# A denoising backbone of two layers on one core: buffers and order of its modulation start, and one weighing run per four attention units

## The chip, the cores and the metric

The kernel runs on one core of one Trainium2 chip. The metric is device time in microseconds (us) of one execution; the median of several runs is told. The engines are TensorE (PE, its weight loads PEld), VectorE (DVE), ScalarE (ACT), GpSimd (POOL) and SyncE (SP), whose queue issues the DMAs here.

## What is computed

The reference runs two layers over 512 latent tokens and 256 context tokens of width 1024, all in float32:

```python
for i in range(DEPTH):
    even = i % 2 == 0
    sh1, sc1, g1, sh2, sc2, g2 = adaln_params(s_x, ada_w[i], ada_b[i])
    h_x = modulate(rms_norm(x, norm1_g[i]), sh1, sc1)
    ...
    if even:
        y_x, y_c = even_mixer(h_x, h_c, attn_w_in[j], ...)   # attention of 12 heads, and Fourier mixing
    else:
        y_x = conformer_conv(h_x, *conv_args)
    x = x + g1 * y_x
    x = x + g2 * sq_relu_mlp(modulate(rms_norm(x, norm2_g[i]), sh2, sc2), mlp_w1[i], mlp_w2[i])
```

`adaln_params` is a product of a conditioning vector with a 1024 x 6144 matrix; `rms_norm` divides by the root of the mean square; attention has 12 query heads on 4 key heads, 512 queries against 768 keys. Only the latent stream is returned.

## The kernel before, in words

Products are made from a high and a low half of each operand, three matmuls for one (`three`, `products`). A weight block of 128 x 2048 comes by DMA into a raw tile of the pool `wraw` (two buffers); its high half is a rounding copy (ACT, line 164 or 363, or POOL, 155 or 962), its low half a subtraction (DVE 158 or 167, POOL 963). `pin` keeps an instruction in program order on its engine; all of the code around the change is pinned, so each engine works in the order in which the code stands.

**The start** (lines 331 to 560). The modulation for layer 0 comes from eight blocks `ar0` to `ar7` (`load_ada`, 339), which alternate between the pool `araw` (two buffers) and `wraw`; between them SP issues the two halves of the latents `xx` and the first two weight blocks (345 to 351). A conditioning step n is `cond_sum` (matmuls 376 over two of the blocks), `cond_copy` (ACT 382), `cond_flip` (transposes 387) and `cond_mods` (six to eight small DVE operations, 395 to 401). Three sides are normed: the context (0) and the two halves of the latents (1, 2). For each: `square` (ACT 406), `fold` (DVE 410, 411), `total` (PE 416), `root` (DVE 422, then Ln and Exp on ACT 423, 424), `newton` (DVE 429 to 431), and then for each of eight row tiles `scaled` (DVE 440), `high` (ACT 444), `low` (DVE 448). `step(side, w, kt, half)` is the projection of one row tile, six matmuls (line 327). The order of it all is written out by hand from line 465 on.

**Attention** (884 to 1023). There are 48 units, each one head and 128 queries; n counts scores and m = n - 3 what is worked off. In an iteration stand: the scores of unit n (PE 572, 574) into one of two banks `sc`, the maximum (DVE 577, 578); the reciprocal and the scaling of unit n - 1's shares (DVE 589, POOL 590); perhaps a `piece` of a weight block (POOL 962, 963); the transposes of unit m (PE 928) and their copies (ACT 933; for odd units the second on DVE, 935); the exponent of unit n with its sum (ACT 584); perhaps a gemv `row` (DVE 231) for later modulations, at the units of `ROWS_AT`; and perhaps weighing. Four units make a group of six weighing steps (`weigh`, PE 946, two matmuls each), put into a list behind the fourth unit. From iteration 12 on, every even m takes three steps from the list. A group's last step is followed by its copy out (ACT 952, DVE 953). The data of two rows is one DMA into `wraw` (`load_rows`, SP 970), whose buffers hold the last two weight blocks until their eight pieces are done.

After attention come the output projection, the MLP, the convolution layer and its MLP, with TensorE all but fully busy.

Of the kernel before, what the change touches and what calls it, by code (L numbers as in the profile page):

```python
# [66 lines left out]
ROWS_AT = (20, 22, 26, 28, 30, 32, 33, 34, 36, 38, 40, 41, 42, 44, 45, 46)  # L67
# [8 lines left out]
def build(tc, xT, ctxT, vec, gbc, rope, dft, dft64, eye, ada1, adat,  # L76
# [211 lines left out]
    with ExitStack() as e1:  # L288
# [27 lines left out]
        def split_k(w):  # L316
            return w.rearrange("p e (k n) -> p e k n", k=4)
# [13 lines left out]
        with ExitStack() as e0:  # L331
            p0 = e0.enter_context(tc.tile_pool(name="p0", bufs=1, side=right, reuse_waits='tile'))
            araw = e0.enter_context(tc.tile_pool(name="araw", bufs=2, side=right, reuse_waits='tile'))
# [5 lines left out]
            def load_ada(n):  # L339
                for k in range(len(araws), n):  # L340
                    a = (araw, wraw)[k % 2].tile([P, WB], F32, name=f"ar{k}", tag="raw")
                    nc.sync.dma_start(a, ada1[k])
                    araws.append(a)
# [36 lines left out]
            def cond_copy(n):  # L380
                sa[n] = p0.tile([P, 512], F32, name="sa", tag="sa", bufs=2)
                pin(nc.scalar.activation(sa[n], pa[n], AF.Copy))
# [30 lines left out]
            def total(slot, a):  # L413
                ps = mbank(slot)[:, :H]
                for i in range(2):
                    pin(nc.tensor.matmul(ps, lhsT=ones, rhs=a[:, i], start=i == 0, stop=i == 1))
                return ps

            def root(ps):
                v = p0.tile([P, H], F32, name="rs_v", tag="rs_v", bufs=2)  # L420
                y = p0.tile([P, H], F32, name="rs_y", tag="rs_y", bufs=2)
                pin(nc.vector.tensor_scalar(v, ps, 1.0 / D, EPS, ALU.mult, ALU.add))
                pin(nc.scalar.activation(y, ps, AF.Ln, bias=eps, scale=1.0 / D))
                pin(nc.scalar.activation(y, y, AF.Exp, scale=-0.5))
                return v, y

# [61 lines left out]
            ps = total(2, b0)  # L488
            cond_copy(1)
            cond_flip(1)  # L490
            cond_mods(1)
            w0 = split_k(ws.take())
            for t in range(4):
                w_high(t)
                pin(sides[0].high(t))
                w_low(t)
                pin(sides[0].low(t))
                step(0, w0, t, 0)
                if t == 1:
                    vy = root(ps)  # L500
                if t == 2:
                    r0 = newton(*vy)
            cond_sum(2, range(8))
            for t in range(4):
                pin(sides[1].scaled(t, r0))
            c0 = square(sides[2].src, 0)
            for t in range(2):
                pin(sides[1].high(t))
            c1 = square(sides[2].src, 4)
            for t in range(2, 4):  # L510
                pin(sides[1].high(t))
            for t in range(4):
                pin(sides[1].low(t))
            cond_copy(2)
            fold(c0, c1)
# [4 lines left out]
            ps = total(3, c0)  # L520
            for t in range(4, 8):
                pin(sides[0].scaled(t, rc))
            for t in range(2, 4):
                step(1, w0, t, 0)
            vy = root(ps)
            w_high(4)
# [6 lines left out]
            cond_sum(3, range(8))  # L533
            cond_copy(3)
# [349 lines left out]
        with ExitStack() as ea:  # L884
# [95 lines left out]
            for n in range(len(units) + AHEAD):  # L980
# [9 lines left out]
                if on and ws.later and m % 2 == 0:  # L990
                    piece()
# [18 lines left out]
                if m in ROWS_AT:  # L1010
                    row()
                if not on:
                    for _ in range(2):
                        if work:
                            weigh(*work.pop(0))
                elif m % 2 == 0:
                    for _ in range(3):
                        if work:
                            weigh(*work.pop(0), True)
# [548 lines left out]
```

## Time and profile before

| | us |
|---|---|
| median of 3 runs (lowest, highest) | 1182.0 (1181.2, 1183.33) |
| the profiled execution | 1180.84 |
| its span in the trace | 1179.1 |
| busy: PE, DVE, ACT, POOL | 1157.3, 762.6, 493.1, 168.7 |
| mean granted TensorE clock | 0.998 of full speed |

In the rows further below a line gives its start, its length, the engine, the source line, what is written from what, and how many instructions are merged in it; in brackets stands how long the engine sat idle before it and what ended that. A weighing step of two matmuls shows as four records. PE's lengths overlap, so distances are best taken from start to start.

### The profile page before, as it was taken

Reading aid. Unit: us, or ns where it says so; the run is one execution under the profiler, and the core shown is the slowest. Engines: PE = TensorE matmul, PEld = TensorE weight load, DVE = VectorE, ACT = ScalarE, POOL = GpSimd, SP = SyncE. Lnnn points to the kernel's source line nnn. Section 1 sums busy time; section 2 is a strip of 40 time slices with the busy share of each in tenths; the row PEclk is TensorE's granted clock in tenths of the full one; section 3 lists DMA queues with packets and bytes.
Section 4 is the critical chain, followed back from the end, with each engine's and each line's share of the span. In section 5 each row is a group of like instructions: output and inputs, shape, how many; then the busy total and the mean of one; then the engine's idle time right before and its main releaser. Section 6 shows DMA issues by size and latency. Waiting matters only on the chain.

```text
span 1179.1 us, 16124 instructions
## 1 busy us (share of the span) xinstructions
PE 1157.3 (98%) x6362; PEld 976.4 (83%) x6362; DVE 762.6 (65%) x1370; ACT 493.1 (42%) x883; POOL 168.7 (14%) x198
## 2 busy tenths in 40 slices
PE   6999999999999999999999999999999999999998
PEld 3688776779988888888889988989988888888887
DVE  4986768878976765665646999899753443443431
ACT  5463787745532331332334423777531331332320
POOL 0202367620000000000011148700000000000000
PEclk9999999999999999999999999999999999999999
DMA  9522103365476455555521425332233223322301
GB/s 373 190 72 62 47 14 131 112 263 198 140 257 246 170 190 211 190 184 197 198 92 68 148 76 190 123 113 103 96 120 107 90 89 107 107 80 99 108 18 54
DMA packets 25339, 160.21 MB, mean 136 GB/s; under 512 B 2608, under 2 KB 5680, under 8 KB 6832
## 3 DMA queue, kind: packets, MB, share of 16 engines
q1 hardware_dynamic: 25264, 159.19, 37.7%
q8 instruction: 50, 0.82, 0.3%
q14 instruction: 25, 0.20, 0.0%
HBM read 157.08 MB, written 2.10 MB: 135 GB/s over the span
## 4 chain that ended last, share of the span: by engine, by line
PE 88%; DVE 7%; ACT 2%; issue 1%; DMA 1%; SPq 1%; POOL 0%; DVEq 0%; ACTq 0%
PE mm L192 25%; PE mm L193 25%; PE mm L191 25%; PE sc L327 3%; PE mm L1219 3%; DVE sm L577 3%; PE po L327 2%; PE po L946 1%; DMA ar<-in_ada 1%; ACT p L584 1%; PE tp L928 1%; PE tp L657 1%; PE sc L572 1%; DVE sm L578 0%; PE sc L574 0%
## 5 line engine op out<-in xcount | busy, mean ns | idle before, releaser
L192 PE MATMUL mm<-act,w 128*128 128x512 f32 (+1 forms) x992 | 338.2, 342 | 0.6 <-DVE act L1401 0.3
L193 PE MATMUL mm<-act,w 128*128 128x512 f32 (+1 forms) x992 | 337.6, 341 | 0.0
L191 PE MATMUL mm<-act,w 128*128 128x512 f32 (+1 forms) x992 | 337.1, 342 | 0.0
L164 ACT ACTIVATE w<-raw 128x1024 fp32r<-128x1024 f32 (+1 forms) x168 | 158.0, 970 | 232.7 <-PE mm L193 205.0
L191 PE MATMUL mm<-f,w 128*128 128x512 f32 (+1 forms) x560 | 207.8, 371 | 0.0
L192 PE MATMUL mm<-f,w 128*128 128x512 f32 (+1 forms) x560 | 207.7, 371 | 0.0
L193 PE MATMUL mm<-f,w 128*128 128x512 f32 (+1 forms) x560 | 207.7, 371 | 0.0
L192 PEld LDWEIGHTS mm<-act,w 128*128 128x128 f32 x992 | 187.8, 190 | 22.7 <-DVE act L1401 1.4
L191 PEld LDWEIGHTS mm<-act,w 128*128 128x128 f32 x992 | 187.2, 190 | 22.3 <-ACT act L1411 0.7
L193 PEld LDWEIGHTS mm<-act,w 128*128 128x128 f32 x992 | 187.8, 190 | 21.1
L167 DVE TENSOR_TENSOR w<-raw,w 128x1024 fp32r<-128x1024 f32 (+2 forms) x168 | 179.5, 1094 | 36.0 <-ACT w L164 27.4
L1107 DVE SCALAR_TENSOR_TENSOR x<-mm,mods,x 128x512 f32<-128x512 f32 (+1 forms) x82 | 55.8, 684 | 170.7 <-PE mm L193 169.8
L1161 DVE TENSOR_TENSOR rsq<-relu 128x512 f32<-128x512 f32 (+1 forms) x76 | 45.6, 606 | 122.8 <-ACT relu L1158 122.8
L1158 ACT ACTIVATE relu<-mm 128x512 f32<-128x512 f32 (+1 forms) x76 | 40.2, 529 | 196.6 <-PE mm L193 194.8
L191 PEld LDWEIGHTS mm<-f,w 128*128 128x128 f32 x560 | 105.5, 188 | 18.3
L192 PEld LDWEIGHTS mm<-f,w 128*128 128x128 f32 x560 | 105.5, 188 | 18.2
L193 PEld LDWEIGHTS mm<-f,w 128*128 128x128 f32 x560 | 105.5, 188 | 17.9
L231 DVE SCALAR_TENSOR_TENSOR gv<-gv,sbc 128x1024 f32<-128x1024 f32 x80 | 96.6, 1225 | 6.1 <-DMA gv<-in_adat 6.1
L167 POOL TENSOR_TENSOR w<-raw,w 128x1024 fp32r<-128x1024 f32 x12 | 29.9, 2515 | 404.4 <-ACT w L164 404.3
L1208 DVE SCALAR_TENSOR_TENSOR sb<-u,vecs,sb 128x512 f32<-128x512 f32 x112 | 75.2, 747 | 0.0
L590 POOL TENSOR_SCALAR p<-p,sm 128x768 f32<-128x768 f32 x48 | 58.8, 1225 | 52.0 <-DVE sm L589 42.0
L584 ACT ACTIVATE p<-sc,sm,rq 128x768 f32<-128x768 f32 x48 | 47.8, 995 | 14.4 <-DVE sm L589 9.7
(235 smaller groups left out, 1283.7 us busy)
## 6 DMA issues: line engine op xcount, KB each, us to landing
raw<-in_w SPq DMA_DIRECT2D x64, 1024.0 KB, 4.8
gv<-in_adat SPq DMA_DIRECT2D x40, 1024.0 KB, 5.1
raw<-in_pw SPq DMA_DIRECT2D x12, 1024.0 KB, 4.9
w<-in_diag SPq DMA_DIRECT2D x8, 1152.0 KB, 5.6
ar<-in_ada SPq DMA_DIRECT2D x8, 1024.0 KB, 10.1
raw<-in_w_in SPq DMA_DIRECT2D x6, 1024.0 KB, 4.9
raw<-in_w_out SPq DMA_DIRECT2D x4, 1024.0 KB, 4.8
xx<-in_xT SPq DMA_DIRECT2D x2, 1024.0 KB, 10.7
```

What stands on the lines that cost most here:

```text
L164: hi = nc.scalar.activation(w[:, 0, r], raw[:, r], AF.Copy)
L167: eng.tensor_tensor(w[:, 1, r], raw[:, r], w[:, 0, r].bitcast(F32), ALU.subtract)
L191: nc.tensor.matmul(ps, lhsT=whi, rhs=xhi, start=first, stop=False)
L192: nc.tensor.matmul(ps, lhsT=whi, rhs=xlo, start=False, stop=False)
L193: nc.tensor.matmul(ps, lhsT=wlo, rhs=xhi, start=False, stop=last)
L231: i = nc.vector.scalar_tensor_tensor(r, r, 1.0, sbc, ALU.mult, ALU.mult, accum_out=mod(l, j, t))
L327: i = nc.tensor.matmul(ps, lhsT=a, rhs=w[:, e, k], start=first, stop=last)
L584: held(on, nc.scalar.activation(p, sc[:, :NK], AF.Exp, bias=sm[:, 1:2], scale=r, accum_out=sm[:, 2:3]))
L590: held(on, nc.gpsimd.tensor_scalar(p, p, sm[:, 3:4], 0.0, ALU.mult, ALU.add))
L1107: nc.vector.scalar_tensor_tensor(xs, ps, mod(l, j, t), xs, ALU.mult, ALU.add)
L1161: nc.vector.tensor_tensor(s, r, r, ALU.mult)
L1208: tap = nc.vector.scalar_tensor_tensor(vs if j == TAPS - 2 else a, u[:, t, j:j + S], w[j], a, ALU.mult, ALU.add)
```

## The change

Three edits. First, the pool `araw` gets a third buffer, and of the eight modulation blocks only 1 and 5 go to `wraw`, so that the first weight block has a `wraw` buffer of its own. Second, the order of the start: `root` is cut into `root_sum` (DVE) and `root_log` (ACT); the first root's sum stands right behind its total, and its Ln, Exp and `newton` behind the first step's loop; two weight high halves stand ahead of that loop and each further one two parts ahead; the `scaled` and `high` of side 1 alternate, the second square comes behind the low halves, `fold` behind `cond_mods(2)`, `total(3)` behind one more part of the step, and `w_high(4)` behind the last `cond_sum`. Third, in attention the weighing list is emptied at every m with m % 4 == 1 (at m = 9 the four steps left, then six each time) in place of three steps at every even m; the eight pieces stand at m = 9, 10, 12 to 22 in place of 10 to 24; and the sixteen rows shift to later units.

```diff
@@ -64,7 +64,8 @@
 SLOTS = ((4, 5, 0, 1, 2, 3), (4, 5, 0, 1), (4, 5, 2, 3))
 PAIRS = (4, 5, 0, 1, 2, 3)
 STEADY = 12
-ROWS_AT = (20, 22, 26, 28, 30, 32, 33, 34, 36, 38, 40, 41, 42, 44, 45, 46)
+ROWS_AT = (22, 24, 26, 28, 30, 32, 34, 36, 38, 40, 42, 44, 45, 46, 46, 47)
+PIECES_AT = (9, 10, 12, 14, 16, 18, 20, 22)
 GV_UP = 4
 GV_OUT = 1
 FOURIER_AT = (-1, 1, 3, 5)
@@ -330,7 +331,7 @@
 
         with ExitStack() as e0:
             p0 = e0.enter_context(tc.tile_pool(name="p0", bufs=1, side=right, reuse_waits='tile'))
-            araw = e0.enter_context(tc.tile_pool(name="araw", bufs=2, side=right, reuse_waits='tile'))
+            araw = e0.enter_context(tc.tile_pool(name="araw", bufs=3, side=right, reuse_waits='tile'))
             cx = p0.tile([P, KT, C], F32, name="cx")
             nc.sync.dma_start(ident, eye)
             nc.sync.dma_start(cx, ctxT)
@@ -338,7 +339,7 @@
 
             def load_ada(n):
                 for k in range(len(araws), n):
-                    a = (araw, wraw)[k % 2].tile([P, WB], F32, name=f"ar{k}", tag="raw")
+                    a = (wraw if k in (1, 5) else araw).tile([P, WB], F32, name=f"ar{k}", tag="raw")
                     nc.sync.dma_start(a, ada1[k])
                     araws.append(a)
 
@@ -416,13 +417,20 @@
                     pin(nc.tensor.matmul(ps, lhsT=ones, rhs=a[:, i], start=i == 0, stop=i == 1))
                 return ps
 
-            def root(ps):
+            def root_sum(ps):
                 v = p0.tile([P, H], F32, name="rs_v", tag="rs_v", bufs=2)
                 y = p0.tile([P, H], F32, name="rs_y", tag="rs_y", bufs=2)
                 pin(nc.vector.tensor_scalar(v, ps, 1.0 / D, EPS, ALU.mult, ALU.add))
+                return v, y
+
+            def root_log(ps, vy):
+                v, y = vy
                 pin(nc.scalar.activation(y, ps, AF.Ln, bias=eps, scale=1.0 / D))
                 pin(nc.scalar.activation(y, y, AF.Exp, scale=-0.5))
                 return v, y
+
+            def root(ps):
+                return root_log(ps, root_sum(ps))
 
             def newton(v, y):
                 r = xp.tile([P, H], F32, name="rstd", tag="rstd", bufs=3)
@@ -486,44 +494,42 @@
             fold(b0, b1)
             cond_sum(1, range(8))
             ps = total(2, b0)
+            v1 = root_sum(ps)
             cond_copy(1)
             cond_flip(1)
             cond_mods(1)
             w0 = split_k(ws.take())
+            w_high(0)
+            w_high(1)
             for t in range(4):
-                w_high(t)
                 pin(sides[0].high(t))
+                if t < 2:
+                    w_high(t + 2)
                 w_low(t)
                 pin(sides[0].low(t))
                 step(0, w0, t, 0)
-                if t == 1:
-                    vy = root(ps)
-                if t == 2:
-                    r0 = newton(*vy)
+            vy = root_log(ps, v1)
+            r0 = newton(*vy)
             cond_sum(2, range(8))
             for t in range(4):
                 pin(sides[1].scaled(t, r0))
+                pin(sides[1].high(t))
             c0 = square(sides[2].src, 0)
-            for t in range(2):
-                pin(sides[1].high(t))
-            c1 = square(sides[2].src, 4)
-            for t in range(2, 4):
-                pin(sides[1].high(t))
             for t in range(4):
                 pin(sides[1].low(t))
+            c1 = square(sides[2].src, 4)
             cond_copy(2)
-            fold(c0, c1)
             for t in range(2):
                 step(1, w0, t, 0)
             cond_flip(2)
             cond_mods(2)
-            ps = total(3, c0)
+            fold(c0, c1)
             for t in range(4, 8):
                 pin(sides[0].scaled(t, rc))
-            for t in range(2, 4):
-                step(1, w0, t, 0)
+            step(1, w0, 2, 0)
+            ps = total(3, c0)
+            step(1, w0, 3, 0)
             vy = root(ps)
-            w_high(4)
             r1 = newton(*vy)
             for t in range(4):
                 pin(sides[2].scaled(t, r1))
@@ -531,6 +537,7 @@
             for t in range(4):
                 pin(sides[2].low(t))
             cond_sum(3, range(8))
+            w_high(4)
             cond_copy(3)
             step(2, w0, 0, 0)
             cond_flip(3)
@@ -987,7 +994,7 @@
                 if last is not None:
                     ready[n - 1] = shares(*last, on)
                     last = None
-                if on and ws.later and m % 2 == 0:
+                if m in PIECES_AT:
                     piece()
                 if m < 0:
                     continue
@@ -1007,16 +1014,15 @@
                     place_query(2, 2 + PLACE_AT.index(m), False)
                 if m == ROWS_AT[0] - 2:
                     load_rows()
-                if m in ROWS_AT:
+                for _ in range(ROWS_AT.count(m)):
                     row()
                 if not on:
                     for _ in range(2):
                         if work:
                             weigh(*work.pop(0))
-                elif m % 2 == 0:
-                    for _ in range(3):
-                        if work:
-                            weigh(*work.pop(0), True)
+                elif m % 4 == 1:
+                    while work:
+                        weigh(*work.pop(0), True)
                 if m % 4 == 3:
                     work += [(pair, half, kt) for kt in range(6)]
             for w_ in work:
```

## Rows read from the trace of the kernel before

**Rows 1.** Windows: length, PE, PEld, DVE, ACT, POOL busy (instructions), clock, DMA share, GB/s.
```profile
260.00:280.00 20.00, 20.00 (x132) 18.37 (x131) 16.10 (x26) 7.13 (x11) 0.00 (x0) 1.00 0.59 211
...
800.00:1179.00 379.00, 375.76 (x1934) 323.12 (x1932) 170.98 (x251) 119.82 (x183) 0.00 (x0) 1.00 0.26 89
```

**Rows 2.** Timeline of the start, TensorE and VectorE, 24 to 56 us.
```profile
24.24 3.09 PE L327 MATMUL po<-w,chl 128*128 128x512 f32 x12 [1.01 <-ACT chl L444]
...
32.20 1.92 PE L376 MATMUL tp<-ar,sT 128*32 128x512 f32 x16
...
34.53 1.22 DVE L410 TENSOR_TENSOR sq<-sq 128x1024 f32<-128x1024 f32 x1
35.79 0.69 DVE L411 TENSOR_TENSOR sq<-sq 128x512 f32<-128x512 f32 x1
...
39.75 0.42 DVE L422 TENSOR_SCALAR rs_v<-sc 128x256 f32<-128x256 f32 x1
...
43.62 0.73 PE L327 MATMUL sc<-w,act 128*128 128x512 f32 x2 [0.64 <-ACT act L444]
...
50.25 5.60 PE L327 MATMUL po<-w,chl 128*128 128x512 f32 x24
```

**Rows 3.** Chain that ended last: start, length, engine and line; copies of the start.
```profile
27.12 0.52 ACT w L363
27.64 0.40 ACT chl L444
```

**Rows 4.** Timeline of the start, the late loads and their last reader.
```profile
16.36 14.62 SPq L342 DMA_DIRECT2D ar<-in_ada x4
...
41.05 1.92 PE L376 MATMUL tp<-ar,sT 128*32 128x512 f32 x16
```

**Rows 5.** Timeline of attention: weighing runs, one unit, one wait for a bank.
```profile
161.44 1.52 PE L946 MATMUL po<-PT,vS 128*64 128x256 f32 x12
...
167.62 0.50 PE L572 MATMUL sc<-kA,qT 128*128 128x512 f32 x1
...
168.42 0.82 PE L928 MATMUL tp<-ident,p 128*128 128x128 f32 x6
...
168.69 0.96 DVE L577 TENSOR_REDUCE sm<-sc 128x1 f32<-128x768 f32 x1 [1.81 <-PE sc L574]
...
169.00 0.48 PE L572 MATMUL sc<-kA,qT 128*128 128x512 f32 x1
...
169.96 0.99 ACT L584 ACTIVATE p<-sc,sm,rq 128x768 f32<-128x768 f32 x1 [0.30 <-PE sc L574]
...
170.66 1.52 PE L946 MATMUL po<-PT,vS 128*64 128x256 f32 x12
...
172.11 0.50 PE L572 MATMUL sc<-kA,qT 128*128 128x512 f32 x1
...
215.64 0.99 ACT L584 ACTIVATE p<-sc,sm,rq 128x768 f32<-128x768 f32 x1 [0.73 <-DVE sm L589]
...
216.78 0.19 PEld L572 LDWEIGHTS sc<-kA,qT 128*128 128x128 f32 x1 [0.18 <-ACT p L584]
...
244.27 3.34 PE L946 MATMUL po<-PT,vS 128*64 128x256 f32 x28
```

**Rows 6.** Chain that ended last: two weighing runs one round apart.
```profile
195.40 1.45 PE po L946 x12
...
204.61 1.45 PE po L946 x12
```

**Rows 7.** Timeline of attention: a gemv row, and a weight piece.
```profile
195.95 1.21 DVE L231 SCALAR_TENSOR_TENSOR gv<-gv,sbc 128x1024 f32<-128x1024 f32 x1
...
163.10 0.61 POOL L962 CAST w<-raw 128x512 fp32r<-128x512 f32 x1
...
163.80 1.28 POOL L963 TENSOR_TENSOR w<-raw,w 128x512 fp32r<-128x512 f32 x1
```

**Rows 8.** Timeline behind attention: the first residual add.
```profile
254.18 0.75 DVE L1107 SCALAR_TENSOR_TENSOR x<-mm,mods,x 128x512 f32<-128x512 f32 x1 [0.80 <-DMA x<-in_xT]
```

## The prediction

> **What bounds the kernel now.** I read the windows first: TensorE is busy for 375.76 of the last 379 us [rows 1], so nothing behind attention can give time back to a change that lies ahead of it, and what the two edited stages cost or save goes to the end almost whole. Then the timeline of the first 50 us: there TensorE still waits, 1.01 us ahead of the first projection step and again inside it [rows 2], because this step alternates with ScalarE and VectorE, and the Ln, Exp and refinement of the first latent root stand in its middle. Then one attention round of four units. Its period shows in the starts of the weighing runs: 170.66 - 161.44 = 9.22 us [rows 5], and 204.61 - 195.40 = 9.21 us where two gemv rows were done in the round [rows 6]. So those rows, 1.21 us of VectorE each [rows 7], cost that round nothing: each is issued beside a weighing run, when VectorE has no score to reduce.
>
> **The start, part by part.** Up to the second conditioning sum nothing changes: the loads ahead of it go out in the same order. *The third buffer* takes the last conditioning load off its wait. Today the four late loads occupy SP from 16.36 for 14.62 us [rows 4]; the last one shares its buffer with the first weight block and waits until that is used. With own buffers it goes out in one stream with the rest, some three us sooner. But its reader, the last conditioning sum, starts at 41.05 and shows no wait for a DMA [rows 4]: priced at 0. The second weight block moves up on SP as well, and its first copy stands behind the third root at about 41: 0 again.
>
> *High halves first, Ln and Exp after the loop.* Today the first step runs from 24.24 to 32.20, 7.96 us, for 24 matmuls; where nothing holds them, 24 take 5.60 [rows 2]. With the halves made ahead, ScalarE has 4 x (0.52 + 0.40) = 3.7 us of copies to do [rows 3], from the conditioning's copy at about 22.5 on, and the root no longer stands among them. So the step should end near 24.24 + 5.6 = 29.8: 2.4 us gained there. TensorE goes on with the third conditioning sum, 1.92 us [rows 2], two parts of the next step, 2.8, and turns the conditioning: done near 34.95. VectorE, by the lengths of the same operations today, has by then made its low parts, the refinement and the four scalings, near 32.3, and waits.
>
> *What is late next.* The fold of the squares stood ahead of the conditioning's reductions on VectorE, from 34.53 to 36.48 [rows 2]. Now it stands behind them, and they wait for the turn. With 0.6 us for them the fold runs from 35.6 to 37.5, a us later than today. The total that needs it is queued on TensorE after one part of a step (to 36.3), so TensorE waits about 1.3 us. Behind the fold VectorE has four scalings, to 39.1, and only then the next root's first operation, at 39.75 today [rows 2]. From there the chain of root, scaling, high half and step is the old one, 43.62 - 39.75 = 3.87 us [rows 2]: the third step starts at 43.0 instead of 43.62. The weight copy that moved behind the last sum is queued on ScalarE ahead of that sum's own copy and holds the last turn by 0.3. At 50.25 [rows 2] 0.3 us are left of 2.4. The bounds: a gain of 2.4 if the fold does not bind, a loss of 1 if the moved copy costs its 0.52 and the fold some more. I take **-0.3**, since each later point of the walk is tied to a row.
>
> **Attention, part by part.** One unit's chain [rows 5]: its score matmuls occupy TensorE for 168.42 - 167.62 = 0.80 us, and with the transposes a unit takes 169.00 - 167.62 = 1.38. The reduction starts 1.07 after the score, the exponent 1.27 after the reduction, and where TensorE did wait for an exponent, the next score in that bank began 216.78 - 215.64 = 1.14 after the exponent's start. So a score holds its bank for 1.07 + 1.27 + 1.14 = 3.48 us, and there are two banks. Today the next score in the same bank comes 172.11 - 167.62 = 4.49 us later [rows 5], as a weighing run lies between: 1.0 us to spare.
>
> *The change* puts all weighing of four units behind the second unit of each four, and four scores follow one another. Count from the end of a weighing run: score 1 at 0, score 2 at 1.38, and at 2.76 TensorE is ready for score 3, whose bank is free at 3.48: it waits **0.72**. Score 4: ScalarE has exponent 1 from 2.34, 0.99 long, and a copy of 0.5 ahead of exponent 2, which starts at 3.82; the bank is free at 4.96; with its transposes TensorE is done at 6.34. *The run*: 12 records last 1.52, 28 last 3.34 [rows 5], so a further record costs 0.114, and a run that takes 1.45 to the next score (172.11 - 170.66) takes 2.82 with 24, against 2.90 for two. With 0.05 to enter it the round is **9.2 us**, as today. The waits for VectorE's copies that lengthen today's round are gone; the waits for the banks stand in their place.
>
> *The gemv rows* turn from hidden to exposed. They now stand at units 22, 24, 26 and so on, and in each round one falls on the unit right behind the weighing run, on VectorE between reduction 1 and reduction 2. Reduction 1 ends near 2.05, two small operations at 2.2, the row, 1.21 [rows 7], at 3.42. Reduction 2 could have begun at 2.46; exponent 2 now starts at 3.42 + 1.27 = 4.69 instead of 3.82, score 4 at 5.83 instead of 4.96. Queued behind the row are reduction 2, the copy of transposed shares and, through them, exponent 2 and score 4. The round becomes **10.1 us, +0.87**. Rounds with a row in that place and scores to their end are those of units 22, 26, 30, 34 and 38: 5 x 0.87 = 4.35. The second row of a round falls later, just ahead of the weighing run, and costs nothing more.
>
> *The weight pieces* on GpSimd are a conversion and a subtraction, 0.70 + 1.28 = 1.98 us [rows 7]. In four scores on end the share scaling of score 1's unit stands behind a piece; it is done near 6.2, and its transposes, wanted at 4.96 + 0.80, wait 0.45. Four rounds have pieces. Bounds 0 and 1.8 for all; I take 1.6. *Taken away:* today one round holds rows at 33 and 34, three rows instead of two; of a row's 1.21 I give back half, 0.6.
>
> *The ends.* The last rows stand at 46, 46, 47 instead of 44, 45, 46. The data of the last two goes into a buffer that the row at 44 frees, and the last copy of transposed shares is queued behind the wait for it; 0 to +1, and I take 0.2, since four of six steps of the last run come before they need that copy. On SP the loads of the third output block, of a gemv pair and of x are held behind those rows, x some 2.5 us more. Today VectorE waits for x until 254.18 [rows 8], and TensorE, which has other banks to write, is busy for all of 260 to 280 [rows 1]: 0, and with that cover gone 2.5.
>
> Sum: -0.3 + 4.35 + 1.6 - 0.6 + 0.2 = +5.25 us. The profiled execution took 1180.84 us (span 1179.1 and 1.7 around it), so 1186.1 by its measure. It lies 1.2 us under the median of the three runs, 1182.0, and the result is a median: the forecast is **1187.3 us**.
>
> **A rule that speaks for the change.** By the rows one run in place of two saves 0.08 us a round [rows 5]. The Trainium skill (TensorEngine Tiling (Array Packing), Key Properties) says that a switch of the tiling mode drains TensorE, and half-width tiles are what the weighing uses. By that rule each round with one entry and one exit fewer is faster. The trace agrees in kind, with those 0.08; the first rival is where such savings would win.
>
> **The rivals.** (1) *The longer run wins, and the banks do not bind.* If the banks come free in time, a round is TensorE's bare work, 4 x 1.38 + 2.82 = 8.34, 0.88 under today's; over ten rounds, with the rows still charged, about -4: **1178**. It decides at a bank loop of 2.76 us instead of 3.48. For it: the waits for copies do vanish. Against it: no link of the 3.48 is idle time. Chance 0.1. (2) *The rows stay hidden*, because VectorE or ScalarE has slack that I don't count: the 4.35 goes, **1183**. Reduction 2 would have to be wanted 0.96 us later than 2.46. Against it: only the copy ahead of exponent 2 gives slack, 0.09. Chance 0.17. (3) *The start keeps its 2.4 us*, the fold being early enough: **1185.2**. Chance 0.08. (4) *The waits compound*: a late exponent 2 also delays the round's later shares and the second row, 0.6 us more in six rounds: **1191**. Chance 0.15. (5) The forecast: 0.5.
>
> **How the numbers follow.** About 0.2%, 2.4 us, is what a measurement can tell. Faster is rival 1, 0.1; the same is rival 2 and the near edge of rival 3, 0.2; slower is the rest, 0.7. The range leaves out rival 1 and the upper part of rival 4: 1181.5 to 1191.5.
>
> **What would show it.** In the changed kernel's rounds: score matmuls (line 572) that wait about 0.7 us for ScalarE's exponent (584), and a second such wait of up to 0.9 where a row stands between two reductions; weighing runs of 24 records, 10.1 us apart from unit 25 to 41 and 9.2 to 9.7 before that. In the start: the first step over near 30, TensorE then waiting for the fold (411) from about 36.3 to 37.6, and the run of 24 that stands at 50.25 within 0.5 us of its place. The forecast is wrong if rounds with rows stay at 9.2, or if that run starts before 49.

## The result, and the profile after

The changed kernel takes 1188.25 us (median) beside 1181.2 us for the kernel before, a ratio of 1.0052 with an interval of 1.004 to 1.0063: slower by about 6 us. One of its five executions, at a granted clock of 0.65, took 1644 us and is left out of the ratio. The forecast was 1187.3 us, its range 1181.5 to 1191.5. The profiled execution took 1187.33 us, its span 1185.5.

In the changed kernel line numbers of attention stand 7 higher and those of the start 1 to 8 higher: the score matmul is L579, the exponent L591, the weighing L953, the share scaling on GpSimd L597, the gemv row L232, the fold L411 and L412.

The 6.4 us between the two spans, 1185.5 - 1179.1, split at two points that both traces have: the unbroken run of 24 that stands at 50.25 before [rows 2], and the first matmul of the output projection, which before is

```profile
247.55 0.50 PE L191 MATMUL mm<-act,w 128*128 128x512 f32 x1
```

| us | before | after | difference |
|---|---|---|---|
| start of the first projection step | 24.24 | 25.65 | +1.41 |
| from there to the run of 24 | 26.01 | 25.87 | -0.14 |
| from the run of 24 to the output projection's first matmul | 197.30 | 202.65 | +5.35 |
| the rest of the span | 931.5 | 931.3 | -0.2 |

The start, from the timeline of the changed kernel (start, length, engine, line, operation; in brackets the idle time ahead of it and what ended it):

```profile
25.65 5.85 PE L328 MATMUL po<-w,chl 128*128 128x512 f32 x24 [1.00 <-ACT chl L452]
...
36.18 0.60 PE L388 MATMUL tp<-ident,sa 128*128 128x128 f32 x4
...
36.82 0.17 DVE L396 TENSOR_REDUCE cmod<-tp 128x4 f32<-128x16 f32 x1 [3.14 <-PE tp L388]
...
37.38 1.22 DVE L411 TENSOR_TENSOR sq<-sq 128x1024 f32<-128x1024 f32 x1
38.64 0.69 DVE L412 TENSOR_TENSOR sq<-sq 128x512 f32<-128x512 f32 x1
...
39.38 1.13 PE L417 MATMUL sc<-sq,ones 128*128 128x256 f32 x4 [1.21 <-DVE sq L412]
...
40.83 0.42 DVE L423 TENSOR_SCALAR rs_v<-sc 128x256 f32<-128x256 f32 x1
...
51.52 5.60 PE L328 MATMUL po<-w,chl 128*128 128x512 f32 x24
```

The first step is unbroken now, 5.85 us instead of 7.96. VectorE then idles 3.14 us for TensorE's turn of the conditioning, and behind it does the reductions and, last, the fold; TensorE waits 1.21 us for that fold. The last line is the run of 24.

Why the first step itself begins later is in the windows (length, busy time of PE, PEld, DVE, ACT and POOL, granted clock, share of the DMA engines, GB/s):

```profile
16.00:20.00 4.00, 1.22 (x12) 0.34 (x16) 3.12 (x6) 0.88 (x1) 0.00 (x0) 0.80 1.01 426
20.00:24.00 4.00, 4.00 (x14) 1.87 (x11) 0.17 (x1) 1.63 (x3) 0.00 (x0) 0.50 1.04 391
24.00:28.00 4.00, 3.00 (x14) 2.08 (x13) 3.57 (x11) 2.92 (x7) 0.00 (x0) 0.85 1.04 437
```

From 18.41 to 25.24 us TensorE was granted 0.50, its lower level of 1.2 GHz; in the kernel before this lasted from 17.94 to 21.35. The matmuls that lead up to the first step lie in that stretch; what it costs is worked out further below.

Attention: two rounds from the chain that ended last, then what lies between two weighing runs in the timeline.

```profile
195.98 2.74 PE po L953 x24
206.02 2.74 PE po L953 x24
216.07 2.74 PE po L953 x24
```

```profile
198.65 0.50 PE L579 MATMUL sc<-kA,qT 128*128 128x512 f32 x1
...
199.73 0.96 DVE L584 TENSOR_REDUCE sm<-sc 128x1 f32<-128x768 f32 x1
...
200.87 1.21 DVE L232 SCALAR_TENSOR_TENSOR gv<-gv,sbc 128x1024 f32<-128x1024 f32 x1
200.97 0.99 ACT L591 ACTIVATE p<-sc,sm,rq 128x768 f32<-128x768 f32 x1
...
202.00 0.95 DVE L584 TENSOR_REDUCE sm<-sc 128x1 f32<-128x768 f32 x1
202.11 0.50 PE L579 MATMUL sc<-kA,qT 128*128 128x512 f32 x1 [0.42 <-ACT p L591]
...
203.26 0.99 ACT L591 ACTIVATE p<-sc,sm,rq 128x768 f32<-128x768 f32 x1 [0.72 <-DVE sm L596]
...
204.40 0.51 PE L579 MATMUL sc<-kA,qT 128*128 128x512 f32 x1 [0.36 <-ACT p L591]
204.59 1.21 DVE L232 SCALAR_TENSOR_TENSOR gv<-gv,sbc 128x1024 f32<-128x1024 f32 x1
204.77 1.81 POOL L597 TENSOR_SCALAR p<-p,sm 128x768 f32<-128x768 f32 x1 [0.47 <-DVE sm L596]
```

The rounds are 206.02 - 195.98 = 10.04 and 10.05 us long, against 9.21 in [rows 6]. Score 1 starts at 198.65, its exponent at 200.97, and score 3 in the same bank at 202.11: 3.46 us, 1.14 of it behind the exponent's start. The row at 200.87 stands between two reductions; the second begins when the row ends, its exponent at 203.26, and score 4 another 1.14 later. Over all of attention's rounds these waits are one line of the groups (160 to 250 us; busy us, mean ns, idle us ahead of them by releaser):

```profile
L579 PE MATMUL sc<-kA,qT 128*128 128x512 f32 x34 | 16.8, 493 | 6.0 <-ACT p L591 5.6
```

The same group of the kernel before has none:

```profile
L572 PE MATMUL sc<-kA,qT 128*128 128x512 f32 x33 | 16.1, 488 | 0.0
```

There it was transposes and weight loads that waited, for the copies of transposed shares.

The end of attention:

```profile
250.87 1.23 DVE L232 SCALAR_TENSOR_TENSOR gv<-gv,sbc 128x1024 f32<-128x1024 f32 x1
...
251.24 1.51 SPq L1035 DMA_DIRECT2D x<-in_xT  x1
251.44 2.80 PE L953 MATMUL po<-PT,vS 128*64 128x256 f32 x22 [0.47 <-ACT PT L940]
252.02 0.08 DVE L232 DVE_READ_ACCUMULATOR gv<-gv,sbc 128x1 f32 x1
252.02 0.42 DVE L942 COPY PT<-tp 128x256 f32<-128x256 f32 x1
...
254.17 0.50 PE L192 MATMUL mm<-act,w 128*128 128x512 f32 x1
```

The last copy does stand behind a row, and the weighing does not wait for it, since its first steps don't need it. The load of x is issued 2.9 us ahead of the first output matmul, 2.5 us ahead in the kernel before.

### The profile page after: what moved, and what is told of

Read it like the earlier page. It is cut to its first block, busy times and chain, and to the rows that moved or that the text cites. A ratio compares the mean times of both kernels' runs of the same rounds, so it can differ in the third digit from the quotient of the medians.

```text
span 1185.5 us, 16132 instructions
## 1 busy us (share of the span) xinstructions
PE 1156.2 (98%) x6362; PEld 976.9 (82%) x6362; DVE 764.7 (65%) x1370; ACT 494.0 (42%) x883; POOL 171.3 (14%) x198
## 4 chain that ended last, share of the span: by engine, by line
PE 90%; DVE 5%; issue 2%; ACT 1%; DMA 1%; POOL 1%; SPq 1%; DVEq 0%; POOLq 0%; ACTq 0%
PE mm L192 25%; PE mm L193 25%; PE mm L194 25%; PE sc L328 3%; PE po L328 3%; PE mm L1225 3%; PE po L953 3%; DVE sm L584 2%; DMA ar<-in_ada 1%; PE tp L935 1%; PE sc L579 1%; ACT p L591 1%; PE tp L664 1%; PE sc L581 1%; POOL p L597 1%
## 5 line engine op out<-in xcount | busy, mean ns | idle before, releaser
L232 DVE SCALAR_TENSOR_TENSOR gv<-gv,sbc 128x1024 f32<-128x1024 f32 x80 | 96.9, 1226 | 8.7 <-DMA gv<-in_adat 8.6
L597 POOL TENSOR_SCALAR p<-p,sm 128x768 f32<-128x768 f32 x48 | 56.2, 1171 | 59.0 <-DVE sm L596 29.9
L591 ACT ACTIVATE p<-sc,sm,rq 128x768 f32<-128x768 f32 x48 | 47.6, 992 | 12.9 <-DVE sm L596 9.6
```

Of the source, the lines that this page charges most:

```text
L232: i = nc.vector.scalar_tensor_tensor(r, r, 1.0, sbc, ALU.mult, ALU.mult, accum_out=mod(l, j, t))
L591: held(on, nc.scalar.activation(p, sc[:, :NK], AF.Exp, bias=sm[:, 1:2], scale=r, accum_out=sm[:, 2:3]))
L597: held(on, nc.gpsimd.tensor_scalar(p, p, sm[:, 3:4], 0.0, ALU.mult, ALU.add))
```

## The experiments

The periods below are between the starts of the weighing runs at units 9, 13, 17 and so on to 45; each row is one profiled execution. A run's number (e1 to e12) is that of its label.

| us | 9-13 | 13-17 | 17-21 | 21-25 | 25-29 | 29-33 | 33-37 | 37-41 | 41-45 |
|---|---|---|---|---|---|---|---|---|---|
| changed kernel | 8.92 | 9.78 | 9.78 | 10.60 | 10.04 | 10.05 | 10.05 | 10.05 | 9.85 |
| attention alone (e2) | 8.93 | 9.77 | 9.77 | 10.60 | 10.04 | 10.08 | 10.04 | 10.04 | 9.85 |
| rows beside the weighing (e3) | 8.91 | 9.77 | 9.77 | 10.58 | 9.38 | 9.61 | 9.81 | 9.61 | 9.54 |
| short rows (e6) | 8.93 | 9.78 | 9.78 | 9.78 | 9.22 | 9.21 | 9.21 | 9.21 | 9.16 |
| pieces beside the weighing (e7) | 8.36 | 9.93 | 9.92 | 10.76 | 10.04 | 10.04 | 10.02 | 10.04 | 9.85 |
| one-tensor form (e9) | 8.98 | 9.84 | 9.84 | 11.68 | 10.15 | 10.16 | 10.15 | 10.15 | 9.96 |
| pieces early (e12) | 8.35 | 9.22 | 9.21 | 10.06 | 10.06 | 10.05 | 10.04 | 10.04 | 9.86 |

### The two halves apart

The start's edits on the attention of the kernel before, and the reverse. Beside the diff's own hunks nothing differs.

> The start of the changed kernel (third buffer, new order) with the attention of the kernel before. My theory, that the start gains 2.4 us in its first step and gives it back at the fold: within 0.3 us of the kernel before (-0.3), up to +1.3 if, as in the changed kernel's profile, TensorE runs at half clock when the second total is made; the run of 24 projection matmuls that stands at 50.25 us before stands between 49.9 and 51.6. Rival, that the new order loses time by itself and attention is less guilty than counted: 2 to 4 us slower than before, with that run of 24 at 52 or later. Rival, that the gain is kept: 2 us or more faster, run at 48.

Measured: 1182.3 us, ratio 1.0008 [0.9999, 1.0016]. In the profiled execution half clock lasted from 19.58 to 29.82 us and reached into the first step, so its start says little about the order of work; the step begins at 26.59 and the run of 24 at 53.82.

> The attention of the changed kernel (weighing in one run per four units, pieces and rows at new units) with the start of the kernel before. My theory: this part alone makes 5.4 us of the loss, so 1186.5 against 1181.2, ratio 1.0045; rounds of 10.05 us where a row stands behind the weighing run and 9.8 where pieces are made, as in the changed kernel. Rival, that the start holds the larger share: 3 us or less slower. If start and attention each had no effect without the other, both single runs would lie within 1 us of the kernel before.

Measured: 1185.98 us, ratio 1.004 [1.0028, 1.0053]. First step at 24.06, run of 24 at 50.07, the same 26.01 us apart as before; its rounds are those of the changed kernel (table), and from the run of 24 to the output projection it takes 202.69 us against 202.65. So attention's edits carry the loss, and the start's are worth nothing that the times can tell.

### The weighing in three steps again, all else as changed

```
-                elif m % 4 == 1:
-                    while work:
-                        weigh(*work.pop(0), True)
+                elif m % 2 == 0:
+                    for _ in range(3):
+                        if work:
+                            weigh(*work.pop(0), True)
```

> The changed kernel with the weighing alone undone: three steps at every even unit, as before, but pieces and rows at their new units. My theory, that the run of 24 bunches four scores and thereby exposes rows and pieces: rounds of 9.2 to 9.3 us everywhere, 6 us less than the changed kernel, 1181.5 to 1182.5, that is as fast as before. Rival, that the new places of the rows and pieces cost the time whatever the weighing: 1186 or more. No waits of a score for its bank should be left.

Measured: 1180.21 us, ratio 0.9988 [0.9979, 0.9997]. With the rows and pieces in their new places and the weighing in the old one the loss is gone: it comes from four scores on end, not from the new places as such. This execution had half clock only from 12.11 to 15.52, before the start's critical steps: the run of 24 comes 25.80 us behind the first step.

### What the rows cost

> The changed kernel with the sixteen gemv rows moved to the units at which the weighing run is made (two at each of units 21, 25, 29, 33, 37, 41, 45, then 46 and 47), so that VectorE does them while TensorE weighs. My theory, that a row between two reductions holds the second score bank: rounds from unit 25 on fall from 10.05 to 9.2 us and the whole by 4.4 to 5 us against the changed kernel, to about 1183.5. Rival, that the rows are not the cause and the run of 24 itself is what costs: within 1 us of the changed kernel, 1188. In both, the wait of the third score for its bank, 0.4 to 0.7 us a round, stays.

```
-ROWS_AT = (22, 24, 26, 28, 30, 32, 34, 36, 38, 40, 42, 44, 45, 46, 46, 47)
+ROWS_AT = (21, 21, 25, 25, 29, 29, 33, 33, 37, 37, 41, 41, 45, 45, 46, 47)
```

Measured: 1185.64 us, ratio 1.0032 [1.0018, 1.0045]; about half of what was expected came back. The timeline of one weighing run tells why:

```profile
206.46 1.98 POOL L597 TENSOR_SCALAR p<-p,sm 128x768 f32<-128x768 f32 x1 [0.62 <-DVE sm L596]
206.54 1.21 DVE L232 SCALAR_TENSOR_TENSOR gv<-gv,sbc 128x1024 f32<-128x1024 f32 x1
...
207.68 1.83 DVE L232 SCALAR_TENSOR_TENSOR gv<-gv,sbc 128x1024 f32<-128x1024 f32 x1
...
209.44 0.41 DVE L960 TENSOR_TENSOR act<-po,act 128x256 fp32r<-128x256 f32 x1
209.78 0.94 DVE L584 TENSOR_REDUCE sm<-sc 128x1 f32<-128x768 f32 x1
...
212.14 0.50 PE L579 MATMUL sc<-kA,qT 128*128 128x512 f32 x1 [0.81 <-ACT p L591]
```

Two rows want 1.21 + 1.21 = 2.42 us and a run lasts 2.74, but the second row takes 1.83: a share scaling lies beside the pair and itself takes 1.98 instead of 0.91. So the first reduction of the next round starts late, at 209.78, and score 3 waits 0.81. Where the rows stand was right as a cause, but one weighing run does not hide two whole rows. The next run therefore left the rows in their places and took their length away: each multiplies 64 of its 1024 columns, and the other 960 are left out.

```
+        n = 64 if on else D
-        i = nc.vector.scalar_tensor_tensor(r, r, 1.0, sbc, ALU.mult, ALU.mult,
+        i = nc.vector.scalar_tensor_tensor(r[:, :n], r[:, :n], 1.0, sbc[:, :n], ALU.mult, ALU.mult,
```

> The changed kernel with attention's sixteen gemv rows cut to 64 of their 1024 columns each (their sums are of those columns only); order, loads and waits stay. Theory (a row between two reductions costs its round 0.87 us through the score bank, five or six times): the weighing runs of the second half stand 9.2 to 9.4 us apart instead of 10.05, the round at unit 22 falls from 10.6 to 9.8, and the time is 4.0 to 4.9 us under the changed kernel, 1183 to 1184. Rival (the rounds are long because four scores follow one another, and the rows only fill waits): the rounds stay near 10 and the time near 1188. Rival (rows cost their full 1.21 in every round): 1180 to 1181.

Measured: 1182.85 us, ratio 1.0013 [1.0004, 1.0022]. The timeline of one round:

```profile
207.96 0.16 DVE L586 SCALAR_TENSOR_TENSOR sm<-sm,rq 128x1 f32<-128x1 f32 x1
...
208.10 0.20 DVE L233 SCALAR_TENSOR_TENSOR gv<-gv,sbc 128x64 f32<-128x64 f32 x1
...
208.32 0.96 DVE L585 TENSOR_REDUCE sm<-sc 128x1 f32<-128x768 f32 x1
...
209.34 0.50 PE L580 MATMUL sc<-kA,qT 128*128 128x512 f32 x1 [0.42 <-ACT p L592]
...
210.80 0.50 PE L580 MATMUL sc<-kA,qT 128*128 128x512 f32 x1
```

Score 3 still waits 0.42 us, score 4 no more, and the rounds are 9.21 to 9.22 us. Six periods are shorter than in the changed kernel: 10.60 became 9.78, four of 10.04 or 10.05 became 9.21 or 9.22, and 9.85 became 9.16, 0.82 + 3.34 + 0.69 = 4.85 us in all. That is the rows' price, against 4.35 in the prediction.

### What the pieces cost

```
-PIECES_AT = (9, 10, 12, 14, 16, 18, 20, 22)
+PIECES_AT = (9, 9, 13, 13, 17, 17, 21, 21)
```

> The changed kernel with GpSimd's eight weight pieces two at a time at units 9, 13, 17 and 21, beside the weighing run, instead of at units 9, 10, 12, 14 and so on. Theory (a piece ahead of a share scaling delays the transposes by 0.45 us in each round that has one between two scores): the first rounds fall from 9.78 to 9.2 or 9.3, four times, and the time by 1.6 to 2.2 us, to 1186 to 1186.6. Rival (pieces cost nothing; the banks alone make 9.78): the rounds stay at 9.78 and the time at 1188. Rival (two pieces on end, 4 us, reach the next scaling behind the run): the wait moves there, rounds of 9.8 to 10.2, 1188 to 1189.

Measured: 1187.24 us, ratio 1.0045 [1.0031, 1.0059]. The period ahead of unit 13 falls by 0.56 us, and the next three rise by 0.15 each: the third answer, two pieces reach past the run. In this trace a tiny VectorE instruction (L585, one column) took 0.87 or 0.88 us three times where it usually takes 0.16, each time until a GpSimd piece ended. In the changed kernel eleven of these, at the units with pieces, took 0.43 to 0.66: eight until the conversion of a piece ended, three until a share scaling did. That made a new theory: the pieces act through this instruction. It was given a form with one tensor operand:

```
-            held(on, nc.vector.scalar_tensor_tensor(sm[:, 1:2], sm[:, 0:1], -1.0,
-                                                    rq[:, qt, h:h + 1], ALU.mult, ALU.mult))
+            held(on, nc.vector.tensor_scalar(sm[:, 1:2], sm[:, 0:1], rq[:, qt, h:h + 1], -1.0,
+                                             ALU.mult, ALU.mult))
```

> The changed kernel with one small VectorE instruction in another form: the product of a unit's maximum, its scale and -1 (one column) as an operation on one tensor with two scalars instead of one on two tensors. Theory (the weight pieces cost their rounds by holding that instruction: in the changed kernel ten of these, in the stretch with pieces, take 0.43 to 0.66 us instead of 0.16 and end with the GpSimd operation beside them, and a score then waits 0.35 us for the late exponent): all of them take 0.16, the first rounds fall from 9.78 to 9.2 to 9.5, four times, and the time by 1.0 to 2.3 us, to 1186 to 1187.2. Rival (what delays them is the shared buffer port in either form, or the scaling that is queued behind a piece on GpSimd, as the prediction had it): the long ones or the rounds of 9.78 stay, 1188.

Measured: 1189.41 us, ratio 1.0063 [1.0049, 1.0076]. The long instructions are gone, all 48 take 0.19 to 0.22 us, and the rounds with pieces are 9.84 us, no shorter. For the changed kernel the theory falls. The wait has only moved:

```profile
182.73 1.28 POOL L970 TENSOR_TENSOR w<-raw,w 128x512 fp32r<-128x512 f32 x1
...
184.00 1.79 POOL L597 TENSOR_SCALAR p<-p,sm 128x768 f32<-128x768 f32 x2
184.24 0.21 DVE L585 TENSOR_SCALAR sm<-sm,rq 128x1 f32<-128x1 f32 x1
...
184.96 0.88 PE L935 MATMUL tp<-ident,p 128*128 128x128 f32 x6 [0.36 <-POOL p L597]
```

The scaling is queued behind the piece, and the transposes wait for the scaling, as the prediction had it. The new form is itself 0.05 us slower, and the rounds are 0.06 to 0.1 longer. The round from unit 21, which has a piece and rows, is longer by 1.08: there the transposes at 196.64 wait 1.32 us for a scaling. Then the pieces were taken out of these rounds altogether:

```
-PIECES_AT = (9, 10, 12, 14, 16, 18, 20, 22)
+PIECES_AT = (1, 2, 3, 4, 5, 6, 7, 8)
```

> The changed kernel with GpSimd's eight weight pieces at units 1 to 8, where the weighing still goes two steps at a time and GpSimd has gaps of 1 to 4 us between two scalings, instead of units 9 to 22. Theory (a share scaling behind a piece makes the rounds of the first half 9.78 us long): with the pieces gone the rounds from units 9, 13 and 17 are 9.2 us, that from unit 21, which has rows, 10.05 instead of 10.6, and the time falls by 1.7 to 2.4 us, to 1185.9 to 1186.5, if the earlier units hide them. Rival (the first rounds are longer for another reason, the places of the queries or the banks): they stay at 9.78 and the time at 1188. Rival (the earlier units do not hide them): the rounds fall to 9.2, but the run at unit 9 begins 1 to 2 us later, 1187.5 to 1188.5.

Measured: 1191.18 us, ratio 1.0087 [1.0072, 1.0102]. The rounds came as expected, 9.22, 9.21 and 10.06; together with the first (8.92 to 8.35) the pieces had cost 39.08 - 36.84 = 2.24 us from unit 9 to unit 25, against 1.6 in the prediction. The time came otherwise: the earlier units do not hide the pieces, and the run at unit 9 begins 110.9 us behind the run of 24 instead of 105.3. GpSimd's gaps there were no slack for TensorE:

```profile
136.23 2.95 POOL L970 TENSOR_TENSOR w<-raw,w 128x512 fp32r<-128x512 f32 x2
...
139.17 1.41 POOL L597 TENSOR_SCALAR p<-p,sm 128x768 f32<-128x768 f32 x1
...
140.63 0.81 PE L935 MATMUL tp<-ident,p 128*128 128x128 f32 x4 [2.44 <-POOL p L597]
```

and the windows of the same stretch show a second price, the granted clock:

```profile
137.00:141.00 4.00, 1.55 (x8) 1.05 (x9) 3.74 (x8) 1.73 (x5) 4.00 (x4) 1.00 0.00 0
141.00:144.40 3.40, 3.40 (x16) 2.03 (x15) 2.19 (x3) 1.95 (x5) 3.32 (x5) 0.50 0.00 0
```

TensorE was busy for 1.55 of 4 us, and behind that it was granted 0.50 for 3.4 us. In the changed kernel it is busy for 3.59 us of the same window and stays at 1.00.

### The start

> The kernel before with the buffers of the change alone: three buffers of their own for the modulation blocks. Theory (no reader of an earlier load is late today): the late loads leave in one stream and end near 22 us instead of 31, and the time is that of the kernel before, within 0.5 us. Rival (a load that comes sooner frees a queue or a buffer on which something waits): 1 us less. Rival (it takes memory traffic from the loads that the first steps need): the first step starts later, up to 1 us more.

```
-            araw = e0.enter_context(tc.tile_pool(name="araw", bufs=2, side=right, reuse_waits='tile'))
+            araw = e0.enter_context(tc.tile_pool(name="araw", bufs=3, side=right, reuse_waits='tile'))
```

(and the blocks' pools as in the change). Measured: 1182.55 us, ratio 1.0006 [0.9997, 1.0015]. The late loads occupy SP until 22.6 us instead of 31.0 [rows 4], 8.4 us sooner where the prediction said some three, and the run of 24 stands 26.01 us behind the first step as before: no gain, as priced.

The next run keeps the unbroken first step and puts the fold and the total back where they were:

```
             cond_copy(2)
+            fold(c0, c1)
...
             cond_mods(2)
-            fold(c0, c1)
+            ps = total(3, c0)
...
-            step(1, w0, 2, 0)
-            ps = total(3, c0)
-            step(1, w0, 3, 0)
+            for t in range(2, 4):
+                step(1, w0, t, 0)
```

> Attention as in the kernel before; the start as changed, but with the fold of the squares and the total back ahead of the third conditioning's reductions, as the kernel before has them. Theory (the fold's new place and the two parts queued behind it take back what the unbroken first step gains): TensorE does not wait 1.2 us for the fold, and counted from the start of the first step the unbroken run of 24 begins 24.2 us later instead of the 25.8 to 26.0 of the kernel before and of the changed one: 1179.3 us, 2.0 under the kernel before. Rival (the fold binds nothing; the root's chain does): 25.8 again, 1181 to 1182 as with the start alone. Rival (the stretch at half clock decides): the same 24.2 from the step's start, but the step itself begins up to 2.5 us later, so 1179.5 to 1182, by how long that stretch is.

Measured: 1180.18 us, ratio 0.9988 [0.9979, 0.9996], 1.7 us under its own kernel before. Its profiled execution had half clock from 16.3 to 30.0 us, through the whole first step, so the 24.2 us can't be read there. They can in the next kernel, which joins this start with three weighing steps:

> The changed kernel with two of its edits undone: the fold and the total back in the place they have in the kernel before, and weighing in three steps at every even unit; the unbroken first step, the buffers, and the new places of rows and pieces stay. Theory (what is left of the change after its two costs are taken out is a gain): 24.2 us from the first step to the unbroken run, attention as with three steps, so 1.6 us under that kernel's 1180.2: 1178.6, ratio to the kernel before 0.9975. Rival (the fold binds nothing): 1180.2, ratio 0.9988. Rival (a TensorE that is through the start sooner only waits longer for the next block's copies): between the two, with a wait for a copy between the start and attention that the others don't have.

Measured: 1178.77 us, ratio 0.9979 [0.9969, 0.9988]: faster than both kernels. In its timeline, at full clock throughout the start:

```profile
25.08 5.82 PE L328 MATMUL po<-w,chl 128*128 128x512 f32 x24 [1.46 <-ACT chl L452]
...
36.02 1.11 PE L417 MATMUL sc<-sq,ones 128*128 128x256 f32 x4
...
49.10 5.60 PE L328 MATMUL po<-w,chl 128*128 128x512 f32 x24
```

The total waits for nothing, and the run of 24 comes 24.02 us behind the first step instead of 25.87 in the changed kernel and 25.80 in e4, which differs from this kernel in the fold and the total alone: their place had held 1.8 us.

> The kernel with the fold first and three weighing steps at a time, and the same small instruction in its one-tensor form. Theory (the one half round of 5.35 us at unit 22, where that instruction stands for about 1 us, falls to 4.7): 0.5 to 0.7 us less, 1178.1 to 1178.3. Rival (the row at that unit is what makes it long): 1178.8, no change.

Measured: 1178.82 us, ratio 0.997 [0.9959, 0.998], against a kernel before that was 0.4 us slower in its call than in the last. The long half round of 5.35 us at unit 22 is gone, it takes 4.54, so there the small instruction was the cause. Another of 5.24 stands two half rounds later, where VectorE waits for the row's own load:

```profile
194.76 1.23 DVE L232 SCALAR_TENSOR_TENSOR gv<-gv,sbc 128x1024 f32<-128x1024 f32 x1 [1.31 <-DMA gv<-in_adat]
```

The profile of e4, with the old form, has that wait too (1.24), that of e8 has not. The small instruction is 0.05 us longer everywhere, and in the time there is no change.

## Why the prediction was right, step by step

**The start, -0.3: right in its working, short of one term.** The fold is what came late next. TensorE's wait for it, 1.3 by the walk, is 1.21 us. Counted from the first step, the root's first operation, the third step and the run of 24 came 15.2, 19.05 and 25.87 us later; the walk had 14.9, 18.8 and 25.7. The gain that it set at 2.4 is 26.01 - 24.02 = 1.99 in e8. What it lacked is the +1.41 ahead of the first step, and so the run of 24 stands 1.27 us from its place and not within 0.5. That is the half-clock stretch, 3.4 us in the profiled execution before and 6.8 in the one after. From the last eight matmuls of the second conditioning sum to the first step it takes 4.00 to 4.03 us in the four profiles of the changed start that are at full clock there (e4, e6, e8, e12) and 5.80 in the changed kernel's. By the mean clock of an execution the longer stretch does not come with the change: the kernel before, executed 77 times beside the experiments, shows 0.994 to 1.000, the experiments with the changed start, 79 times, 0.993 to 1.000, and both average 0.998. One thing the walk set at nothing: at full clock the first step waits 1.46 us for its high half (e8) instead of 1.01, as two weight copies in place of one now stand ahead of it on ScalarE. The start alone is 1.0008 [0.9999, 1.0016], from -0.1 to +1.9 us, so the walk's -0.3 lies just outside.

**The bank loop, 3.48 us and a wait of 0.72: right.** It is 3.46 us in the trace. The weight loads of score 3 wait 0.66 us, its matmul, whose sequencing overlaps them, 0.42. A round without rows or pieces is 9.21 us in e6 and 9.22 in e12, where the working had 9.2. That rules out rival 1: it needed rounds of 8.34.

**The weighing run, 2.82: it is 2.74,** to the next score (198.65 - 195.91). Two runs of 12 took 2.90, so one run does save 0.16 a round. The Trainium skill (TensorEngine Tiling (Array Packing), Key Properties) has a switch of tiling mode drain TensorE; the saving agrees in kind. That the drain makes it is not shown, and the banks take it back.

**The rows, +4.35: right in place, low by 0.5.** A round with a row behind its run is 10.04 to 10.08 us where 10.1 was forecast. The prediction counted five such rounds; a sixth, with its last scores near the end (41-45), lost 0.69 too. Rival 2 falls with e6, rival 4 with rounds that stay at 10.05, and rival 3 with the fold's wait.

**The pieces, 1.6: low by 0.6.** The place was right, a scaling queued behind a piece. The transposes were to wait 0.45 us; each of four rounds lost 0.54 to 0.57. So the rounds from unit 13 and 17 are 9.78 us, and that from 21, which has pieces and rows, 10.60, not the 9.2 to 9.7 that was named. In e9 the wait stands at the transposes alone; in the changed kernel it is split between them and a score behind a late exponent, for the same sum.

**The ends, +0.2 and x at no cost: nothing, by one wrong reason.** From the weighing run at unit 45 to the first output matmul it is 8.22 us in the changed kernel and 8.23 with short rows (e6), so the last rows cost that stretch nothing. But x was not held by 2.5 us: on SP it stands ahead of the last gemv load, not behind it. VectorE waits 2.53 us for x instead of 0.80 [rows 8], and TensorE doesn't feel it, as the rest of the span is no longer than before.

**What was given back, 0.6: too little.** The prediction took 9.21 us for every round of the kernel before and gave back 0.6 for the one with rows at 33 and 34. In its trace that round is

```profile
209.04 1.52 PE L946 MATMUL po<-PT,vS 128*64 128x256 f32 x12
...
219.41 1.52 PE L946 MATMUL po<-PT,vS 128*64 128x256 f32 x12
```

219.41 - 209.04 = 10.37 us, 1.16 over 9.21, and the round from 179.88 to 190.60 is 10.72, 1.5 over, since rows and pieces fell on the units 20 and 22 together; a later one loses 0.4. So some 3.0 us of the same kind of loss went away with the change. No run took these out one by one, but e8 has the new places under the old weighing: there these rounds are 9.21, 10.07 and 9.21 us, 2.2 of the 3.0 less, and what is left stands at unit 22, where a piece and a row still meet.

Attention was forecast at 4.35 + 1.6 - 0.6 + 0.2 = +5.55 and came at +5.35. By the measured terms it is 4.85 + 2.24 - 3.0 = 4.1; the other 1.3 us lies ahead of the first and behind the last of these rounds, and how it divides there is open. The sum was nearer than its terms: rows and pieces were 1.1 us too small, what was given back 2.4, and 1.3 lies where 0.2 was expected. That these cancel is luck.

## What to carry to other kernels

Work of a fixed amount that is moved into one block leaves the rest bare: count the loop of each double buffer in the part that no longer has a pause in it, and look at what else lay in the cover that moved away, here the gemv rows and GpSimd's pieces. When a step is made faster, follow every engine to what it waits for next; here a fold on VectorE that was put behind a turn took back 1.8 of 2 us, and its old place gives them. A gap on an engine is slack only if nobody waits for what is queued behind the filler.

## What the runs showed of the hardware

- A GpSimd scaling that meets a gemv row on VectorE takes 1.81 us (204.77 above) instead of 0.91, and 1.98 beside two rows; with rows of 64 columns (e6) their mean over 36 is 0.91. In turn a VectorE instruction of one column with two tensor operands took up to 1.03 us beside a GpSimd piece in the kernel before (188.76 us, the piece ended at 189.77), and with one tensor operand never more than 0.22. The Trainium skill (SBUF — State Buffer, SBUF: two separate sides) has GpSimd and a VectorE operation with two inputs from SBUF share a port pair as an exclusive lock, so that the later one blocks; these numbers agree.
- TensorE's granted clock is a term of the start by itself: stretches at 0.50 between 11 and 30 us, of 0 to 13.7 us in all, differ from execution to execution. In the changed kernel's profile the way to the first step took 5.80 us against 4.00 to 4.03 at full clock, in that of e5 one stretched the step itself to 7.54 us instead of 5.85.
